# The row maximum of the attention scores and its scaling made by one VectorE operation

## The chip, the cores and the metric

The kernel runs on one core of a Trainium2 chip. The metric is the device time of one execution in microseconds; less is better. Before the change the median of three runs is 1622.26 us (1620.82 to 1622.88). The core has a matrix engine (TensorE, PE in the profile), a vector engine (VectorE, DVE), an activation engine (ScalarE, ACT), GpSimd (POOL) and a queue engine (SyncE, SP) that issues all of this kernel's DMAs. Matrix products land in PSUM; everything else on the chip lies in SBUF.

## The reference

Two sequences (x_prompt and x_sample, called A and B here) of 1024 tokens by 1024 features go through the same two layers. The first is a pooling mixer beside an attention with 8 query heads of 64 and 2 key/value heads; the second is a gated layer. What matters here is the softmax:

```python
s = jnp.einsum('bqkgd,bskd->bkgqs', q_blk, k, preferred_element_type=jnp.float32) * scale
p = jax.nn.softmax(s, axis=-1).astype(v.dtype)
return jnp.einsum('bkgqs,bskd->bqkgd', p, v)
```

For each query row the softmax needs the greatest of 1024 scores, subtracts it, takes the exponential and divides by the sum.

## The kernel before, in words

The attention works on pairs of heads: `attention(st, j, rate)` takes head pair j (0 to 3) of one sequence. In it, 8 token tiles (4 groups of two) and two heads make 16 score tiles of 128 queries by 1024 keys. Four pairs and two sequences make 128 score tiles. A's attention begins at about 90 us of the span and B's ends at about 880 us.

`scores` (L673 to L687) makes one tile. Four matmuls of 128x512 (L678) fill a PSUM tile `ps` of 128x1024 in f32; there are two such PSUM tiles (`ps_s`, L213). VectorE takes the maximum of each row (L684, `m`). ScalarE multiplies it by the negative scale `s_neg`, a [128, 1] operand (L685, `nb`). ScalarE then computes exp(scale * ps + nb) with the sum of each row as accumulator output (L686). `ps` is free for the next matmuls when L684 and L686 have read it.

`split` (L689 to L701) handles the tile before it: ScalarE scales the sum (L693), VectorE takes the reciprocal (L695), ScalarE writes the high half of the probabilities in f16 (L697), VectorE the low half (L698), and SyncE issues the DMA that transposes both (L699). `pv` (L703) multiplies them with the values on TensorE (L710) and VectorE evacuates the result (L714).

Between two score tiles `fill(rate)` takes chunks of other work from a list of fillers: the projections of this and the other sequence and the pooling mixer during A's attention, the output projection of A and the beginning of the second layer during B's. Their matmuls are in a helper, L399. Weight blocks are loaded in f32 by SyncE (L153) and split in two f16 halves by ScalarE (L169) and VectorE (L170); the buffers come out of one arena.

Two planners stand around this. `make_plan` (L76) gives each buffer of the arena its place: a first pass notes when each buffer is taken and freed, and the plan then places all of them in `ARENA` bytes per partition, seeking places whose last user is long gone. So a different arena size gives other places and other reuse. And the program is scheduled by the framework (L1060, `schedule_with_timeline_sim=True`), which sets the order on each engine by its own estimate of the timeline; that order is not always the order of the lines.

Of the kernel before, what the change touches and what calls it, by code (L numbers as in the profile page):

```python
# [13 lines left out]
BF16 = mybir.dt.bfloat16  # L14
I32 = mybir.dt.int32
AF = mybir.ActivationFunctionType
ALU = mybir.AluOpType
AX = mybir.AxisListType
PSUM = bass.MemoryType.PSUM

P = 128
L = 1024
# [7 lines left out]
PAD = 8  # L30
W_PAD = L + 2 * PAD
RING = 96
ARENA = 201 * 1024
GRAIN = 512


class Arena:
# [3 lines left out]
    def __init__(self, nc, pool, plan=None):  # L41
        self.tile = pool.tile([P, ARENA // 4], F32, name="arena")
        self.nc, self.plan = nc, plan
        self.spans, self.held, self.now = [], {}, 0.0
# [45 lines left out]
def tried(spans, order, end):  # L90
    placed, plan = [], [None] * len(spans)
    for i in order:
# [3 lines left out]
        holes, last = [], 0  # L96
        for lo, hi in clash + [(ARENA, ARENA)]:
            if lo - last >= g:
# [101 lines left out]
class Kernel:  # L200
    def __init__(self, ctx, tc, args, order, plan):
        self.nc, self.tc, self.order = tc.nc, tc, order
        self.__dict__.update(args)
        self.one = one = ctx.enter_context(tc.tile_pool(name="one", bufs=1))
        self.kept = one.tile([P, 640], F32, name="kept")
        self.kept_at = 0
        self.rings, self.role = {}, "misc"
        self.blocks = {}
        self.arena = Arena(tc.nc, one, plan)
        self.get, self.free = self.arena.get, self.arena.free  # L210
        self.diff = one.tile([P, 2, L], F32R, name="diff")
        self.pw = one.tile([P, 2, 4, P], F32R, name="pw")
        self.ps_s = ctx.enter_context(tc.tile_pool(name="ps_s", bufs=2, space=PSUM))  # L213
        self.ps_g = ctx.enter_context(tc.tile_pool(name="ps_g", bufs=3, space=PSUM))
        self.ps_o = ctx.enter_context(tc.tile_pool(name="ps_o", bufs=1, space=PSUM))
        dram = ctx.enter_context(tc.tile_pool(name="dram", bufs=1, space=bass.MemoryType.DRAM))
        self.x1 = [dram.tile([L, D], F32, name=f"x1_{s}") for s in range(2)]
        self.mixed = [dram.tile([8, P, L], F32, name=f"mixed_{s}") for s in range(2)]
        self.w = {"in_e": self.w_in_e, "out_e": self.w_out_e, "in_o": self.w_in_o, "out_o": self.w_out_o}
        self.fillers = deque()  # L220
        self.credit = 0
        self.turned = {}
# [437 lines left out]
    def attention(self, st, j, rate):  # L660

        nc = self.nc
        while not {("q", j), ("az", j)} <= st.done:
            cost, fn = self.fillers.popleft()
            fn()
            self.credit -= cost
        kv = j // 2
        out = self.get([P, L], F32)
        sz = st.az[j]["t"]
        sc = self.product(st.az[j]["d"], st.dv, 2.0 ** -15, tag="so")  # L670
        pts = {}

        def scores(tt, h):  # L673
            ps = self.ps_s.tile([P, L], F32, name="ps_s")
            for half in range(2):
                for a in range(2):
                    self.arena.now += 512
                    nc.tensor.matmul(out=ps[:, half * 512:half * 512 + 512], lhsT=st.qT[j][:, tt, h, :],  # L678
                                     rhs=st.kT[:, 4 * half:4 * half + 4, kv, a, :], start=a == 0, stop=a == 1)
            m = self.tiny([P, 1])  # L680
            nb = self.tiny([P, 1])
            p = self.pf.get()
            ss = self.tiny([P, 1])
            nc.vector.tensor_reduce(out=m, in_=ps, axis=AX.X, op=ALU.max)  # L684
            nc.scalar.activation(out=nb, in_=m, func=AF.Copy, scale=self.s_neg[:, 0:1])  # L685
            nc.scalar.activation(out=p, in_=ps, func=AF.Exp, scale=self.s_scale[:, 0:1], bias=nb[:, 0:1], accum_out=ss)  # L686
            return p, ss  # L687

        def split(tt, h, p, ss):  # L689
            if tt % 2 == 0:  # L690
                pts[tt // 2, h] = self.pt.get()
            s2 = self.tiny([P, 1])
            nc.scalar.activation(out=s2, in_=ss, func=AF.Copy, scale=2.0 ** -15)  # L693
            r = self.tiny([P, 1])
            nc.vector.reciprocal(out=r, in_=s2)  # L695
            hl = self.phl.get()
            nc.scalar.activation(out=hl[:, 0, :], in_=p, func=AF.Copy, scale=r[:, 0:1])  # L697
            nc.vector.scalar_tensor_tensor(out=hl[:, 1, :], in0=p, scalar=r[:, 0:1], in1=hl[:, 0, :], op0=ALU.mult, op1=ALU.subtract)  # L698
            nc.sync.dma_start_transpose(  # L699
                out=pts[tt // 2, h].rearrange("p a t n -> p (a t) n")[:, :, (tt % 2) * P:(tt % 2 + 1) * P],  # L700
                in_=hl.rearrange("p a n -> p (a n)"))  # L701

        def pv(g):  # L703
            ps = self.bank(self.ps_o)[:, 0:256]
            n = 0
            for t in range(NT):
                for a, b in self.PASSES:
                    for h in range(2):
                        self.arena.now += 128
                        nc.tensor.matmul(out=ps[h * HD:h * HD + HD, :], lhsT=st.v[:, a, t, kv * HD:kv * HD + HD],  # L710
                                         rhs=pts[g, h][:, b, t, :], start=n < 2, stop=n >= 6 * NT - 2)
                        n += 1
            cols = slice(g * 256, g * 256 + 256)
            nc.vector.scalar_tensor_tensor(out=out[:, cols], in0=ps, scalar=sc[:, 0:1], in1=sz[:, cols], op0=ALU.mult, op1=ALU.mult)  # L714

        prev = None
        for g in range(NT // 2):
            for h in range(2):
                for tt in (2 * g, 2 * g + 1):
                    with self.as_role("attention"):  # L720
                        cur = (tt, h) + scores(tt, h)
                        if prev:
                            split(*prev)
                    prev = cur
                    self.fill(rate)
                    if g and h == 1 and tt % 2 == 0:
                        pv(g - 1)
        with self.as_role("attention"):
            split(*prev)
        self.fill(rate)  # L730
        pv(NT // 2 - 1)
        self.amax(st.mam[:, 4 + j:5 + j], out)
        if j < 3:
            nc.sync.dma_start(out=self.mixed[st.s][4 + j], in_=out)
            self.free(out)
        else:
            st.mix[7] = out
        self.free(sz, st.qT.pop(j))
# [348 lines left out]
```

## Time and profile before

| | before |
|---|---|
| median of 3 runs | 1622.26 us |
| profiled execution, its time | 1619.84 us |
| profiled execution, its span | 1618.1 us |
| mean granted TensorE clock, share of full speed | 0.976 |
| PE, DVE, ACT busy over the span | 92%, 66%, 45% |

The span is the time from the first to the last instruction of the profiled execution; 1.7 us lie around it. The busy shares are averages over stages with different limits, so the prediction reads them by stretch.

### The profile page before, as it was taken

What the parts mean: (1) busy time and instruction counts of PE and PEld (TensorE: products, weight loads), DVE (VectorE), ACT (ScalarE), POOL (GpSimd) and SP (SyncE); (2) the same over time, 40 slices, a digit from 0 to 9 for tenths busy, and PEclk for the clock granted to TensorE, in tenths of its full rate; (3) what the DMA queues carried; (4) which work ended last, traced back from release to release, by engine and by line L of the source; (5) the groups of instructions that cost most, each with busy time, mean ns of one, the idle gap of its engine ahead of it and who ended that gap; (6) DMA issues with size and microseconds to landing.
All of it is one profiled execution on the core that took longest, in us unless ns stands there. A gap on an engine that the chain in (4) does not pass through costs nothing.

```text
span 1618.1 us, 28061 instructions
## 1 busy us (share of the span) xinstructions
PE 1496.5 (92%) x11751; PEld 1014.1 (63%) x11751; DVE 1061.8 (66%) x1613; ACT 729.0 (45%) x1121; POOL 117.3 (7%) x187
## 2 busy tenths in 40 slices
PE   2989998878799999999799999999999999998999
PEld 1754654557456787464478887554488554467888
DVE  7899999889897675788975854466650643345211
ACT  4367767767664364566755811133432521111000
POOL 2410000102000000000200100010000200000000
PEclk9999999889889999999899999999999999999999
DMA  9558688899948877675997643157210023114121
GB/s 252 116 118 161 150 148 183 186 210 194 213 87 213 211 156 151 144 154 133 224 260 164 186 125 98 40 157 167 81 40 1 27 66 117 46 66 137 60 85 53
DMA packets 497152, 217.69 MB, mean 135 GB/s; under 512 B 366337, under 2 KB 488705, under 8 KB 497025
## 3 DMA queue, kind: packets, MB, share of 16 engines
q1 hardware_dynamic: 497024, 215.90, 57.0%
q8 instruction: 92, 1.51, 0.4%
q14 instruction: 36, 0.29, 0.1%
HBM read 101.04 MB, written 24.12 MB: 77 GB/s over the span
## 4 chain that ended last, share of the span: by engine, by line
PE 57%; DVE 16%; DMA 11%; issue 4%; ACT 4%; POOL 1%; SPq 1%; DVEq 0%; ACTq 0%; POOLq 0%
PE bank L399 35%; PE ps_s L399 17%; DMA arena<-arena 4%; PE bank L710 3%; DVE arena L698 3%; DVE ring_attention L684 3%; PE ps_s L678 3%; DMA arena<-in_w_in_e 2%; DMA arena<-in_w_in_o 1%; DMA arena<-x 1%; ACT arena L686 1%; DVE ring_weights L252 1%; DVE arena L170 1%; DVE arena L756 1%; DVE arena L622 1%
## 5 line engine op out<-in xcount | busy, mean ns | idle before, releaser
L399 PEld LDWEIGHTS <-arena 128*128 128x128 f16 x9600 | 863.9, 99 | 434.1 <-DMA arena<-arena 25.6
L399 PE MATMUL bank<-arena 128*128 128x256 f16 (+2 forms) x8064 | 941.1, 277 | 31.8 <-ACT arena L169 12.7
L399 PE MATMUL ps_s<-arena 128*128 128x512 f16 x1536 | 338.1, 380 | 2.4 <-DVE arena L170 2.4
L169 ACT ACTIVATE arena<-arena,kept 128x1024 f16<-128x1024 f32 x108 | 121.4, 1142 | 281.1 <-DVE kept L281 126.2
L170 DVE SCALAR_TENSOR_TENSOR arena<-arena,kept 128x1024 f16<-128x1024 f32 x108 | 137.6, 1288 | 80.9 <-ACT arena L169 63.9
L698 DVE SCALAR_TENSOR_TENSOR arena<-arena,ring_attention 128x1024 f16<-128x1024 f32 x128 | 163.2, 1278 | 31.3 <-ACT arena L697 29.9
L684 DVE TENSOR_REDUCE ring_attention<-ps_s 128x1 f32<-128x1024 f32 x128 | 155.0, 1216 | 10.8 <-PE ps_s L678 10.5
L697 ACT ACTIVATE arena<-arena,ring_attention 128x1024 f16<-128x1024 f32 x128 | 145.5, 1141 | 36.0 <-DVE ring_attention L695 27.1
L678 PE MATMUL ps_s<-arena 128*128 128x512 f16 x512 | 136.8, 394 | 26.2 <-ACT arena L686 21.5
L686 ACT ACTIVATE arena<-ps_s,ring_attention,kept 128x1024 f32<-128x1024 f32 x128 | 153.7, 1201 | 8.4 <-DVE ring_attention L695 3.7
L784 DVE SCALAR_TENSOR_TENSOR arena<-bank,ring_dout,arena 128x512 f32<-128x512 f32 x64 | 47.9, 749 | 149.7 <-PE bank L399 149.7
L710 PE MATMUL bank<-arena 128*64 128x256 f16 x1536 | 107.7, 290 | 35.7 <-DMA arena<-arena 34.3
L710 PEld LDWEIGHTS <-arena 128*64 128x64 f16 x1536 | 90.2, 117 | 61.2 <-DMA arena<-arena 31.6
L252 DVE TENSOR_REDUCE ring_weights<-arena 128x1 f32<-128x1024 f32 x58 | 70.2, 1215 | 66.6 <-DMA arena<-in_w_in_o 29.4
L678 PEld LDWEIGHTS <-arena 128*128 128x128 f16 x512 | 47.9, 100 | 81.1 <-issue 38.6
L685 ACT ACTIVATE ring_attention<-ring_attention,kept 128x1 f32<-128x1 f32 x128 | 37.1, 290 | 131.4 <-DVE ring_attention L684 131.0
L364 DVE SCALAR_TENSOR_TENSOR arena<-arena,ring_norm 128x1024 f32<-128x1024 f32 x32 | 41.8, 1306 | 25.7 <-POOL ring_norm L318 22.7
L362 ACT ACTIVATE arena<-arena 128x1024 f32<-128x1024 f32 x32 | 33.7, 1054 | 53.1 <-DMA arena<-x 32.9
L903 DVE TENSOR_TENSOR arena<-arena 128x1024 f32<-128x1024 f32 x16 | 19.6, 1223 | 51.2 <-ACT arena L902 51.2
L838 ACT ACTIVATE arena<-bank,ring_dvv 128x256 f32<-128x256 f32 x64 | 26.7, 466 | 54.8 <-PE bank L399 53.9
L902 ACT ACTIVATE arena<-ps_s,ring_duz 128x1024 f32<-128x1024 f32 x16 | 17.7, 1109 | 66.8 <-PE ps_s L399 66.8
L365 ACT CAST arena<-arena 128x1024 f16<-128x1024 f32 x32 | 33.2, 1037 | 23.8 <-DVE arena L364 22.3
(104 smaller groups left out, 883.6 us busy)
## 6 DMA issues: line engine op xcount, KB each, us to landing
arena<-in_w_in_o SPq DMA_DIRECT2D x48, 512.0 KB, 4.4
arena<-in_w_in_e SPq DMA_DIRECT2D x36, 512.0 KB, 4.8
arena<-in_w_out_e SPq DMA_DIRECT2D x16, 512.0 KB, 4.6
x<-arena SPq DMA_DIRECT2D x32, 256.0 KB, 3.0
arena<-x SPq DMA_DIRECT2D x16, 512.0 KB, 4.8
arena<-x SPq DMA_DIRECT2D x32, 256.0 KB, 3.0
out<-arena SPq DMA_DIRECT2D x32, 256.0 KB, 2.1
mixed<-arena SPq DMA_DIRECT2D x14, 512.0 KB, 4.1
```

The source lines that it names most:

```text
L169: nc.scalar.activation(out=hi, in_=raw, func=AF.Copy, scale=s[:, 0:1])
L170: nc.vector.scalar_tensor_tensor(out=lo, in0=raw, scalar=s[:, 0:1], in1=hi, op0=ALU.mult, op1=ALU.subtract)
L252: self.nc.vector.tensor_reduce(out=out, in_=in_, axis=axis, op=ALU.max, apply_absolute_value=True)
L364: nc.vector.scalar_tensor_tensor(out=x, in0=x, scalar=r[:, 0:1], in1=gain[0], op0=ALU.mult, op1=ALU.mult)
L399: self.nc.tensor.matmul(out=o, lhsT=l, rhs=r, start=first and i == 0, stop=last and i == n - 1)
L678: nc.tensor.matmul(out=ps[:, half * 512:half * 512 + 512], lhsT=st.qT[j][:, tt, h, :], rhs=st.kT[:, 4 * half:4 * half + 4, kv, a, :], star ...
L684: nc.vector.tensor_reduce(out=m, in_=ps, axis=AX.X, op=ALU.max)
L686: nc.scalar.activation(out=p, in_=ps, func=AF.Exp, scale=self.s_scale[:, 0:1], bias=nb[:, 0:1], accum_out=ss)
L697: nc.scalar.activation(out=hl[:, 0, :], in_=p, func=AF.Copy, scale=r[:, 0:1])
L698: nc.vector.scalar_tensor_tensor(out=hl[:, 1, :], in0=p, scalar=r[:, 0:1], in1=hl[:, 0, :], op0=ALU.mult, op1=ALU.subtract)
L710: nc.tensor.matmul(out=ps[h * HD:h * HD + HD, :], lhsT=st.v[:, a, t, kv * HD:kv * HD + HD], rhs=pts[g, h][:, b, t, :], start=n < 2, stop=n ...
L784: nc.vector.scalar_tensor_tensor(out=res, in0=ps.rearrange("p (t n) -> p t n", t=2), scalar=box["d"][:, 0:1], in1=res, op0=ALU.mult, op1=A ...
```

## The change

VectorE no longer makes a plain maximum. One `tensor_scalar` multiplies each score by the negative scale, takes the lesser of the product and 3e38 (which changes nothing), and keeps the least of the results in its accumulator output, which is `nb`. As `s_neg` is negative, the least product is the product of the greatest score. The elementwise result goes to a scratch tile of 128x1024 in bf16 that nobody reads; its 2 KB per partition are taken from the arena. The ScalarE multiplication (L685) goes. The [128, 1] tile `m` goes too.

```diff
-ARENA = 201 * 1024
+ARENA = 199 * 1024
...
+        self.scratch = one.tile([P, L], BF16, name="scratch")
...
-            m = self.tiny([P, 1])
             nb = self.tiny([P, 1])
             p = self.pf.get()
             ss = self.tiny([P, 1])
-            nc.vector.tensor_reduce(out=m, in_=ps, axis=AX.X, op=ALU.max)
-            nc.scalar.activation(out=nb, in_=m, func=AF.Copy, scale=self.s_neg[:, 0:1])
+            nc.vector.tensor_scalar(out=self.scratch, in0=ps, scalar1=self.s_neg[:, 0:1], scalar2=3.0e38, op0=ALU.mult, op1=ALU.min, accum_out=nb)
             nc.scalar.activation(out=p, in_=ps, func=AF.Exp, scale=self.s_scale[:, 0:1], bias=nb[:, 0:1], accum_out=ss)
```

## Rows read from the trace of the kernel before

**Rows 1.** Page, part 1: busy us, share of the span, instructions.
```profile
PE 1496.5 (92%) x11751; PEld 1014.1 (63%) x11751; DVE 1061.8 (66%) x1613; ACT 729.0 (45%) x1121; POOL 117.3 (7%) x187
```

**Rows 2.** Stretch, its length; busy PE, PEld, DVE, ACT, POOL; granted clock; DMA.
```profile
90.00:290.00 200.00, 184.55 (x1373) 103.08 (x1371) 188.20 (x314) 142.45 (x246) 11.94 (x20) 0.99 0.77 155
290.00:480.00 190.00, 160.96 (x1458) 107.04 (x1457) 168.41 (x256) 134.00 (x224) 25.72 (x35) 0.91 0.89 181
480.00:880.00 400.00, 373.73 (x3098) 261.63 (x3097) 300.00 (x425) 229.16 (x381) 20.67 (x38) 0.98 0.79 179
880.00:1618.00 738.00, 722.45 (x5294) 499.30 (x5292) 334.23 (x465) 187.81 (x225) 28.38 (x48) 0.99 0.30 88
```

**Rows 3.** The chain of waits from 90 to 880 us, shares by line.
```profile
by line: PE bank L399 25.3%; DMA arena<-arena 7.8%; issue 7.8%; DVE arena L698 6.1%; PE bank L710 5.8%; DVE ring_attention L684 5.7%; PE ps_s L678 5.7%; DMA arena<-in_w_in_e 4.2%; ACT arena L686 2.9%; DVE arena L622 1.9%; DMA arena<-in_w_ou
```

**Rows 4.** The chain in order of time: start, us, what; L684's and L685's first and last.
```profile
90.92 1.13 DVE ring_attention L684
...
181.16 1.23 DVE ring_attention L684
...
182.41 0.30 ACT ring_attention L685
...
756.02 0.19 ACT ring_attention L685
...
818.50 1.14 DVE ring_attention L684
```

**Rows 5.** Groups by line: xcount | busy us, mean ns | idle before, releasers.
```profile
L684 DVE TENSOR_REDUCE ring_attention<-ps_s 128x1 f32<-128x1024 f32 x128 | 155.0, 1216 | 10.8 <-PE ps_s L678 10.5
L685 ACT ACTIVATE ring_attention<-ring_attention,kept 128x1 f32<-128x1 f32 x128 | 37.1, 290 | 131.4 <-DVE ring_attention L684 131.0
L686 ACT ACTIVATION_READ_ACCUMULATOR arena<-ps_s,ring_attention,kept 128x1 f32 x128 | 24.5, 191 | 0.0
L695 DVE RECIPROCAL ring_attention<-ring_attention 128x1 f32<-128x1 f32 x128 | 19.9, 157 | 19.6 <-ACT ring_attention L693 19.3
L591 DVE SCALAR_TENSOR_TENSOR arena<-arena,bank 128x512 f32<-128x512 f32 x32 | 21.7, 679 | 1.4 <-ACT arena L590 1.4
L884 DVE SCALAR_TENSOR_TENSOR arena<-bank,kept,arena 128x512 f32<-128x512 f32 x32 | 22.8, 748 | 31.3 <-PE bank L399 31.2
L753 DVE TENSOR_SCALAR arena<-arena,kept 128x1024 f16<-128x1024 f32 x16 | 11.2, 747 | 0.1
```

**Rows 6.** Timeline from 242 us: start, us, engine, line, operation.
```profile
243.00 1.22 DVE L684 TENSOR_REDUCE ring_attention<-ps_s 128x1 f32<-128x1024 f32 x1
244.13 1.27 DVE L698 SCALAR_TENSOR_TENSOR arena<-arena,ring_attention 128x1024 f16<-128x1024 f32 x1
244.58 1.20 ACT L686 ACTIVATE arena<-ps_s,ring_attention,kept 128x1024 f32<-128x1024 f32 x1
245.68 0.19 ACT L686 ACTIVATION_READ_ACCUMULATOR arena<-ps_s,ring_attention,kept 128x1 f32 x1
245.77 1.14 ACT L169 ACTIVATE arena<-arena,kept 128x1024 f16<-128x1024 f32 x1
```

**Rows 7.** DVE's runs of L684 in the first stretch.
```profile
90.00:290.00 200.00, 49.76 (x41) 0.99 0.77 155
```

**Rows 8.** Waits: who waited for whom, us in total, times, longest.
```profile
PE ps_s L678 <- ACT arena L686: 21.5, 14, 3.0
SPq L699 <- DVE ring_attention L684: 55.6, 14, 6.7
SPq L153 <- DVE arena L170: 86.0, 13, 21.3
```

**Rows 9.** Timeline at 569 us, and the chain's weight loads between 90 and 880 us.
```profile
569.70 2.35 DVE L684 TENSOR_REDUCE ring_attention<-ps_s 128x1 f32<-128x1024 f32 x2
93.27 5.10 DMA arena<-in_w_in_e
...
827.60 4.16 DMA arena<-in_w_in_o
```

## The prediction

> **What bounds the kernel now.** I read the page's totals first, then the busy time by stretch, then the chain of waits, then the groups and a piece of the timeline for prices. Over the whole span TensorE is busy 92% and VectorE 66% [rows 1], which would make VectorE a bystander. The stretches say otherwise. From 90 to 290 us, the first part of A's attention, VectorE is busy 188.2 of 200 us, and from 290 to 480 us 168.4 of 190; in B's attention (480 to 880 us) it is 300 of 400, with TensorE at 373.7; after 880 us TensorE has 722 of 738 us to itself [rows 2]. So 128 score tiles lie in a region of 790 us, where A's half leaves VectorE 11.8 + 21.6 = 33 us of idle time and B's half leaves TensorE 26 us. In the last stretch the change touches nothing but places of buffers.
>
> The chain of waits from 90 to 880 us is mixed: TensorE's fillers have 25%, transposes 8%, and the reduction L684 has 5.7%, which is 45 us of 790 [rows 3]. In order of time the chain holds L684 in 47 pieces, the first at 90.9 and the last at 818.5 us; 38 of them are whole runs of 1.07 to 1.24 us. It holds L685, the multiplication that goes, in 19 pieces from 182.4 to 756.0 us, 4.1 us together (ten of about 0.30, the rest shorter) [rows 4]. That is the quantity to see: ScalarE's 128 runs of 290 ns are 37.1 us of busy time [rows 5], but only 4.1 us of it is on the path.
>
> **The change part by part.** *What ScalarE loses.* 128 x 290 ns = 37.1 us of ScalarE work [rows 5]. ScalarE is busy 142 of 200, 134 of 190 and 229 of 400 us in the three stretches [rows 2], so most of this is idle time traded for idle time. On the path it is worth the 4.1 us above, and one hop of about 0.02 us (the gap from 182.39 to 182.41 us [rows 4]) in each of the ten places where the chain goes from L684 straight into L685: 0.2 us. I take -4.3 us, and keep 0 as the small end, because a parallel wait may be right behind. At the other end, the exp that frees a PSUM tile starts about 0.3 us earlier, and TensorE waited for that exp 14 times [rows 8]: 14 x 0.3 = 4.2 us more, were VectorE to charge nothing for it.
>
> *What VectorE gains in work.* No row shows a `tensor_scalar` that reads PSUM with an accumulator output, so it is bounded from its neighbours. The reduction over 1024 takes 1216 ns and the next operation starts 1.13 us after it began (243.00 to 244.13) [rows 6]. The operand `s_neg` is read per partition: the same operation on 512 elements in which PSUM takes part takes 679 ns with a constant (L591) and 748 ns with a [128, 1] operand (L884) [rows 5], so I add 0.06 to 0.07 us, and take 0.06. The accumulator has to be brought out. VectorE shows no such step anywhere in this trace; ScalarE does, as an instruction of its own of 191 ns [rows 5], which started 1.10 us into its exp and let the next operation start 0.09 us later (244.58, 245.68, 245.77) [rows 6]. VectorE's nearest [128, 1] operation, the reciprocal, takes 157 ns [rows 5]. Low end: the accumulator comes out within the operation, 0, and a score tile costs 0.06 us more. High end: no overlap at all, 1.28 + 0.19 = 1.47 us where the step was 1.13, so 0.34 more. The row it is nearest to is ScalarE's, with 0.09 to 0.19 us: I take 0.13, and so 0.19 us more per tile, 24 us of VectorE's time over 128 tiles. There is an end below nothing too: a `tensor_scalar` from SBUF over 1024 elements takes 747 ns (L753) [rows 5]. If the new one ran at that rate from PSUM, a tile would cost 0.47 - 0.13 = 0.34 us less; it is priced among the rivals.
>
> The Trainium skill (VectorE: DVE Perf Modes, Two Vector instructions with no wait between them) says that an operation that also writes out its accumulator is two instructions, the main one and an accumulator read. ScalarE's rows agree in kind; no VectorE row here shows it. By that rule the low end of 0.06 us falls away and the sum is the one I take or above it; by the low end alone the forecast would be no change.
>
> *Where that work lies.* On the chain: 38 whole runs x 0.19 = +7.2 us. Beside the chain: in the first stretch VectorE makes 41 of the 128 reductions [rows 7], 12 of the 38 are there, so 29 are not on the chain; but they would add 29 x 0.19 = 5.5 us to an engine with 11.8 us idle [rows 2]. VectorE's order is fixed, and SyncE sits for 55.6 us, 14 times, at a transpose (L699) until an L684 has run [rows 8]; so what is late on VectorE makes transposes late, and with them L710. I count half of it: +2.8 us. Elsewhere I count nothing beside the chain: the fillers cover it, and if they don't, the other 61 runs off the chain (128 - 41 - 26) cost up to 61 x 0.19 = 11.6 us.
>
> *Waits.* The exp now waits for VectorE itself and not for L685; behind it on ScalarE stand the same instructions as stood behind L685. The scratch tile is written by VectorE alone, so no other engine waits for it. No DMA is added or moved.
>
> *Arena and order.* 2 KB of 201 go, so the planner places every buffer anew, and the framework orders the engines anew (already now it puts two reductions of consecutive tiles one behind the other at 569.70 us, which the lines don't have [rows 9]). Both can gain or lose. Weight loads are the place: 12 of them are on the chain between 90 and 880 us, 3.6 to 5.6 us each, 55 us together [rows 9], and their issue waited 86 us, 13 times, for L170 to have read the buffer before [rows 8]. One load more or less on the path is some 4.5 us either way. I take 0 for the value and keep both ends.
>
> *Sum.* -4.3 + 7.2 + 2.8 = +5.7 us against the profiled execution's 1619.84 us, which gives 1625.5; the median of the runs is 2.4 us above it, so the prediction is 1622.26 + 5.7 = 1628 us. With VectorE's low end it is -4.3 + 38 x 0.06 + 29 x 0.06 / 2 = -1.1 us; with its high end -4.3 + 38 x 0.34 + 29 x 0.34 / 2 = +13.5 us.
>
> **The rivals.** *ScalarE's relief decides (faster).* The accumulator costs VectorE nothing, and each exp, 0.3 us earlier, frees its PSUM tile earlier: -4.3 - 4.2 + 38 x 0.06 = -6.2 us, 1616 us. For it speak the 21.5 us that TensorE waited for L686 [rows 8], which is the largest wait of L678 for an engine; against it, that VectorE at 94% [rows 2] can't start the reduction earlier. It wins over the forecast from a price below about 0.08 us a tile on VectorE. Chance 0.22.
>
> *Both sides cancel (no change).* The longer operation still hands over sooner: 1.19 + 0.19 + 0.02 us from its start to the exp against 1.23 + 0.02 + 0.30 + 0.02 before [rows 4]. At the ten places where the chain goes through L685 that is already in the sum; if fillers cover the 28 others by half, the result is -4.3 + 10 x 0.19 + 14 x 0.19 = 0.3 us, 1622.5 us. Chance 0.22.
>
> *The new places decide (slower).* Two weight loads or transposes more on the path, 9 to 10 us, beside the forecast's +5.7: 1637 us. For it speaks that the issues already wait for buffers; against it, that it may fall the other way. Chance 0.12.
>
> *The new operation runs at the double rate (much faster).* 0.34 us less on 38 + 14 runs and 4.3 on ScalarE: -17.7 - 4.3 = -22 us, 1600 us. For it speaks L753; against it, that L884 and L591 with an operand in PSUM take 1.3 to 1.5 ns an element, as an operation at the single rate and its start would. The Trainium skill (VectorE: DVE Perf Modes, Why PSUM operands drop a tier) says that a 32-bit operand in PSUM keeps an operation at one element a cycle; no row here has a `tensor_scalar` from PSUM to show it. Chance 0.04.
>
> **How the numbers follow.** The forecast has the rest, 0.40, with its own range of 1623 to 1634 us. A measurement of this kernel can tell about 0.2%, 3.2 us, from no change. Faster: 0.22 + 0.04 = 0.26. Same: 0.22 and about 0.05 of the forecast, whose lower edge lies inside that band, 0.27. Slower: 0.35 + 0.12 = 0.47. The range is 1612 to 1639: it leaves out the double rate, and the tails of the first and third rivals, some 0.15 to 0.2 together.
>
> **What would show it.** Right: a VectorE operation of about 1.28 us at L681 and beside it a second, short one, 128 times; VectorE's busy time up by some 20 us or more; ScalarE's down by about 37; VectorE above 95% from 90 to 290 us, and TensorE's idle time there up, not down. Wrong: no second instruction, or an exp that starts less than 1.3 us after the VectorE operation with TensorE's waits for L686 gone; or VectorE as forecast but the difference lying after 880 us or in weight loads, which would be the places. A time under 1619 us would say that ScalarE was on the path by more than its pieces of the chain.

## The result and the profile after

The changed kernel takes 1647.18 us (median of four runs, 1646.47 to 1647.48) against 1622.57 us for the kernel before in the same session. The ratio is 1.015, interval 1.0135 to 1.0165: 24.6 us slower. The forecast of 1628 us had the sign right, but the time lies outside its range, which ended at 1639.

The profiled execution took 1647.43 us, with a span of 1645.7 us and a mean granted TensorE clock of 0.961 (before 1618.1 us and 0.976). First the page's totals, which answer to [rows 1]:

```profile
PE 1508.8 (92%) x11751; PEld 1019.5 (62%) x11751; DVE 1071.1 (65%) x1741; ACT 698.4 (42%) x993; POOL 115.7 (7%) x187
```

TensorE executes the same 11751 matmuls and is busy 12.3 us longer with them. The other 15.3 us of the 27.6 are TensorE idle. VectorE has 128 instructions more and only 9.3 us more busy time; ScalarE has 128 less and 30.6 us less.

The groups by line, which answer to L684 to L686 in [rows 5] (lines are shifted by one: the exp is L685 now, the low half's L698 is L697, the helper's L399 is L400):

```profile
L684 DVE TENSOR_SCALAR_CACHE_REDUCE scratch<-ps_s,kept 128x1024 bf16<-128x1024 f32 x128 | 163.3, 1275 | 12.7 <-PE ps_s L679 12.0
L684 DVE DVE_READ_ACCUMULATOR scratch<-ps_s,kept 128x1 f32 x128 | 10.5, 82 | 0.0
L685 ACT ACTIVATE arena<-ps_s,ring_attention,kept 128x1024 f32<-128x1024 f32 x128 | 153.6, 1200 | 136.3 <-DVE scratch L684 127.4 <-DVE arena L697 4.5 <-DVE ring_attention L694 2.9
```

The new operation is two instructions on VectorE, 1275 and 82 ns, as the prediction said in kind. The timeline shows what they cost a neighbour; it answers to [rows 6]. Three dots stand for rows of other engines that are left out:

```profile
338.98 1.27 DVE L684 TENSOR_SCALAR_CACHE_REDUCE scratch<-ps_s,kept 128x1024 bf16<-128x1024 f32 x1
...
340.18 0.08 DVE L684 DVE_READ_ACCUMULATOR scratch<-ps_s,kept 128x1 f32 x1
340.18 1.28 DVE L697 SCALAR_TENSOR_TENSOR arena<-arena,ring_attention 128x1024 f16<-128x1024 f32 x1
340.30 1.20 ACT L685 ACTIVATE arena<-ps_s,ring_attention,kept 128x1024 f32<-128x1024 f32 x1 [1.32 <-DVE scratch L684]
```

The accumulator is read from 340.18 us on, 1.20 us after the operation began, and the next VectorE operation starts in the same instant. So the step from one operation to the next is 1.20 us where it was 1.13 [rows 6]: 0.07 us a tile. The 128 tiles of the two traces agree: the median step is 1.203 us for 1.134, and in 107 of them the next operation starts with the read. And the exp starts 1.32 us after VectorE began, where it was 1.23 + 0.02 + 0.30 + 0.02 = 1.57 us [rows 4].

These rows account for at most 128 x 0.07 = 9 us of VectorE's time, most of it beside other work, and not for 25 us. The stretches, against [rows 2], show where the time is lost:

```profile
90.00:290.00 200.00, 194.66 (x1410) 109.29 (x1409) 187.83 (x358) 129.77 (x199) 13.89 (x18) 0.97 0.76 153
290.00:480.00 190.00, 143.69 (x1292) 96.54 (x1290) 159.08 (x271) 125.08 (x191) 23.04 (x35) 0.83 0.93 187
480.00:880.00 400.00, 371.19 (x3025) 252.63 (x3024) 306.51 (x475) 209.47 (x315) 22.15 (x41) 0.96 0.75 168
880.00:1645.00 765.00, 745.89 (x5516) 519.47 (x5513) 348.35 (x489) 199.84 (x245) 26.01 (x48) 0.99 0.31 90
```

From 90 to 290 us TensorE issues even more than before (1410 matmuls for 1373). From 290 to 480 us it falls back: 143.7 us busy for 161.0, 1292 matmuls for 1458. The mean granted clock of that stretch is 0.83 of 2.4 GHz (before 0.91), so more of it ran at the lower level, 1.2 GHz, with TensorE idle 46 us of 190. VectorE too does less there, 159.1 for 168.4 us. The last of the 128 reductions starts at 894.2 us where it was 872.2: 22 of the 27.6 us are lost by the end of attention, and 15.8 of them by the 64th reduction (438.9 us for 423.1), where A's score tiles end. The largest wait of the score matmuls for an engine has doubled (before 21.5 us, 14 times [rows 8]):

```profile
PE ps_s L679 <- ACT arena L685: 42.6, 19, 6.4
```

Two things changed, then: the operation, and the 2 KB that the scratch tile takes from the arena, which moves the buffers and gives the framework another problem to order. The experiments take them apart.

### The profile page after: what moved, and what is told of

It reads as the page before. It is cut to its first block, busy times and chain, and to the rows that moved or that the text cites. A ratio compares the mean times of both kernels' runs of the same rounds, so it can differ in the third digit from the quotient of the medians.

```text
span 1645.7 us, 28017 instructions
## 1 busy us (share of the span) xinstructions
PE 1508.8 (92%) x11751; PEld 1019.5 (62%) x11751; DVE 1071.1 (65%) x1741; ACT 698.4 (42%) x993; POOL 115.7 (7%) x187
## 4 chain that ended last, share of the span: by engine, by line
PE 54%; DVE 19%; DMA 14%; issue 5%; ACT 5%; POOL 2%; SPq 2%; DVEq 0%; ACTq 0%; POOLq 0%
PE bank L400 34%; PE ps_s L400 15%; DMA arena<-arena 4%; DVE scratch L684 4%; DMA arena<-in_w_in_e 3%; DVE arena L697 3%; PE bank L709 3%; DVE arena L170 2%; PE ps_s L679 2%; DMA arena<-in_w_in_o 2%; ACT arena L685 1%; ACT arena L169 1%; DVE arena L365 1%; DMA arena<-in_w_out_e 1%; DVE ring_weights L253 1%
## 5 line engine op out<-in xcount | busy, mean ns | idle before, releaser
L400 PEld LDWEIGHTS <-arena 128*128 128x128 f16 x9600 | 869.3, 99 | 442.4 <-DMA arena<-arena 25.6
L400 PE MATMUL bank<-arena 128*128 128x256 f16 (+2 forms) x8064 | 948.2, 279 | 31.1 <-ACT arena L169 13.2
L400 PE MATMUL ps_s<-arena 128*128 128x512 f16 x1536 | 337.7, 380 | 8.2 <-ACT arena L169 8.1
L685 ACT ACTIVATE arena<-ps_s,ring_attention,kept 128x1024 f32<-128x1024 f32 x128 | 153.6, 1200 | 136.3 <-DVE scratch L684 127.4
L679 PE MATMUL ps_s<-arena 128*128 128x512 f16 x512 | 142.1, 404 | 49.9 <-ACT arena L685 42.6
L697 DVE SCALAR_TENSOR_TENSOR arena<-arena,ring_attention 128x1024 f16<-128x1024 f32 x128 | 163.1, 1278 | 16.7 <-ACT arena L696 16.6
L684 DVE TENSOR_SCALAR_CACHE_REDUCE scratch<-ps_s,kept 128x1024 bf16<-128x1024 f32 x128 | 163.3, 1275 | 12.7 <-PE ps_s L679 12.0
L253 DVE TENSOR_REDUCE ring_weights<-arena 128x1 f32<-128x1024 f32 x58 | 70.5, 1216 | 68.8 <-DMA arena<-in_w_in_o 32.6
L367 DVE TENSOR_TENSOR arena<-arena 128x1024 f16<-128x1024 f32 x32 | 39.9, 1250 | 4.9 <-ACT arena L366 4.9
L316 POOL TENSOR_SCALAR ring_norm<-ring_norm 128x1 f32<-128x1 f32 x32 | 12.8, 400 | 422.6 <-ACT arena L363 418.3
```

The source lines that it names most:

```text
L253: self.nc.vector.tensor_reduce(out=out, in_=in_, axis=axis, op=ALU.max, apply_absolute_value=True)
L400: self.nc.tensor.matmul(out=o, lhsT=l, rhs=r, start=first and i == 0, stop=last and i == n - 1)
L684: nc.vector.tensor_scalar(out=self.scratch, in0=ps, scalar1=self.s_neg[:, 0:1], scalar2=3.0e38, op0=ALU.mult, op1=ALU.min, accum_out=nb)
```

## The experiments

Ratios are to the kernel before on the same chip, with the 95% interval.

### The places alone

```diff
-ARENA = 201 * 1024
+ARENA = 199 * 1024
```

That is the kernel before, with the maximum and the product on ScalarE as they were.

> The kernel before with only the arena cut to 199 KB; TENSOR_REDUCE and the ScalarE product stay, no scratch tile. If the new operation is what costs (theory O), this stays at 1622 us (within 3). If the new places of the buffers, and the order that follows from them, cost it (theory P), this is at 1640 to 1650 us, as the changed kernel. A share of both would lie between, and says how much each has.

1.0175 (1.0151 to 1.0199), 1653.72 us. The arena by itself costs all that the change costs. The same stretches of its profile:

```profile
90.00:290.00 200.00, 193.11 (x1399) 107.42 (x1397) 184.65 (x316) 140.81 (x242) 11.78 (x17) 0.98 0.76 149
290.00:480.00 190.00, 150.35 (x1369) 102.92 (x1367) 158.49 (x236) 131.66 (x222) 24.79 (x35) 0.88 0.94 192
480.00:880.00 400.00, 360.13 (x2903) 243.47 (x2902) 295.88 (x417) 215.59 (x361) 26.18 (x41) 0.95 0.74 166
```

It is like the changed kernel in kind: ahead in the first stretch, TensorE down to 150.4 us in the second, a lower granted clock. It does not lose the time in the same place, though: its 64th reduction starts 8.4 us later than before (431.5 us) and its last 26.4 us later (898.6), so that two thirds of its loss lie in B's attention, where TensorE is busy 360.1 of 400 us for 373.7. Its score matmuls wait more too, without the new operation:

```profile
PE ps_s L678 <- ACT arena L686: 34.2, 15, 5.0
```

Three more sizes, each the kernel before with one number changed. For 203 KB the 2 KB come from rings of small values (next experiment).

```diff
-ARENA = 201 * 1024
+ARENA = 198 * 1024    # the others: 200, 203
```

> The kernel before with an arena of 198 KB: another draw of places. If an arena of less than 201 KB costs because there is less of it, this is slower than e1. If places and order are a lottery, it lies anywhere within some 10 us of e1 or of 1622 us.

198 KB: 1.0173 (1.0151 to 1.0195), 1653.86 us.

> The kernel before with an arena of 200 KB. The planner places all buffers at the first attempt, as at 201 and 203 KB, and 72 of 593 lie elsewhere than at 201. At 199 and 198 KB two 4 KB buffers of a weight block (taken at 49% of the run) find no hole; they are put ahead of the others and all is placed again, so that 340 of 593 lie elsewhere. Theory R (that second attempt costs, not the space): 1622 to 1630 us. If time goes with space: about half of e1's +28, 1636 to 1642 us.

200 KB: 1.0046 (1.0028 to 1.0064), 1636.06 us.

> The kernel before with an arena of 203 KB (the 2 KB from rings whose slots are never used twice). If it is the amount of space that counts, this is at 1622 us or faster. If each plan is a draw, and that of 201 KB a good one, this is slower by 10 to 30 us, like 199 and 198 KB.

203 KB: 1.0004 (0.999 to 1.0018), 1626.74 us. So it is not a slope: 201 and 203 KB agree, 200 costs 0.5%, 199 and 198 cost 1.7%. (198 is no independent draw: one buffer of 593 lies elsewhere than at 199.)

### The operation without the loss of memory

The scratch tile's 2 KB come out of rings of [128, 1] values whose slots are never used twice, and the arena stays at 201 KB. The plan is then the same as before, buffer for buffer; only the operation differs.

```diff
+            size = RING if self.role in ("attention", "norm", "rope", "misc", "weights") else 32
...
-ARENA = 199 * 1024
+ARENA = 201 * 1024
```

> The changed kernel with the arena left at 201 KB; the 2 KB for the scratch tile come from the rings of [128, 1] values whose slots are never used twice. The plan of places is that of the kernel before. Theory O: 1640 to 1650 us, as the changed kernel. Theory P: near the prediction's price of the operation alone, 1622 to 1630 us.

1.0057 (1.0036 to 1.0078), 1636.89 us: about a third of the loss. But the framework orders the engines anew around the changed operation, so this isn't yet the operation's own price. The same at 198 KB, to be read against 198 KB with the old operations:

> The changed kernel's operation with an arena of 198 KB. Against e3 it gives the operation's effect under another draw of places: theory O says +20 to +25 us over e3, theory P +0 to +8 us, and a lottery of the order says any difference, of either sign.

1.0151 (1.0131 to 1.0172) for 1.0173: here the operation seems to gain 0.2%, and the changed kernel itself against the places alone gives 1.015 for 1.0175, the same sign; both differences lie within the intervals. So the order had to be held fixed.

### The operation in the old order

The program is scheduled with the old operations; afterwards each of the 128 reductions is replaced in its place on VectorE by the new operation, with the waits on its own engine that the scratch tile needs. In the first kernel ScalarE still makes its product; in the second the product goes as well, and the exp takes over its wait. The lines are those of the second kernel; in the first, the traces show every instruction of TensorE, ScalarE and GpSimd in the order of the kernel before:

```diff
+            if type(ins).__name__ == "InstTensorReduce" and ins.ins[0].memref.startswith("ps_s"):
+                l[i] = mybir.InstTensorScalarPtr(
...
+                    ins=(ins.ins[0], by, mybir.ImmediateValue(dtype=F32, value=3.0e38)),
+                    outs=(scratch, out), op0=ALU.mult, op1=ALU.min)
```

> The kernel before with its places and its order on every engine kept, instruction by instruction; only the 128 reductions are replaced, after the order is set, by the new multiply-and-keep-the-least operation (by -0.5, with its scratch tile and its waits on itself). The ScalarE multiplication stays and multiplies by twice the scale. So only VectorE's price is added, 0.06 us and the 0.08 us accumulator read of the changed kernel's profile. Theory O (the operation's own price makes e2's +11 us): +8 to +14 us over before. Theory S (the new order makes it): +0 to +6 us, the prediction's sum for VectorE alone being 38 x 0.14 + 29 x 0.14 / 2 = 7 us at most.

1.0024 (1.001 to 1.0038), 1629.29 us, that is +3.9 us. Here VectorE multiplies by a constant and ScalarE still multiplies by the scale, so only VectorE pays.

> As e5, and the ScalarE multiplication is taken out too, its waits moved to the exp: the whole change of the computation, with the places and the order of the kernel before. The prediction's sum without any new order is +2 to +4 us (0.14 us a tile on the chain, less 4.3 us of ScalarE). Theory S: at or below 1622 us within 3. Theory O: +8 to +14 us, as e2.

1.0006 (0.9995 to 1.0018), 1628.01 us for 1626.02. Against the kernel before it in this pair, ScalarE's product is worth 0.18%, some 2.9 us. The whole change, without new places and a new order, is no change that can be measured. VectorE's groups have the durations of the changed kernel, and the handover on VectorE is the same:

```profile
244.52 1.28 DVE L685 TENSOR_SCALAR_CACHE_REDUCE arena<-ps_s,kept 128x1024 bf16<-128x1024 f32 x1
...
245.72 0.08 DVE L685 DVE_READ_ACCUMULATOR arena<-ps_s,kept 128x1 f32 x1
245.72 1.28 DVE L699 SCALAR_TENSOR_TENSOR arena<-arena,ring_attention 128x1024 f16<-128x1024 f32 x1
```

The exp starts 1.40 us after the operation began, where it was 1.32 in the changed kernel (1.41 and 1.32 in the median), so that this kernel takes a little less of ScalarE's relief than it could.

The wait of the score matmuls is back at its old size, and so is TensorE from 290 to 480 us (160.1 us busy for 161.0 [rows 2]):

```profile
PE ps_s L679 <- ACT arena L687: 20.1, 14, 3.0
```

```profile
290.00:480.00 190.00, 160.09 (x1438) 106.75 (x1439) 166.88 (x280) 127.33 (x194) 27.57 (x38) 0.89 0.90 182
```

VectorE is busier in this stretch than in the changed kernel (166.9 us for 159.1), with the same operation. So the operation, as such, doesn't make that stretch slow.

### What about the places

At 203, 201 and 200 KB the planner's first attempt fits. At 199 and 198 KB two buffers of 4 KB, halves of one weight block, find no hole. The planner puts each at the front of its list and places everything again, twice; in the end 340 of 593 buffers lie elsewhere than at 201 KB (72 at 200 KB, 21 at 203). Two experiments on this theory (R: the restart is the loss). First another set of places at 201 KB, by another value of the planner's limit for how long a place should have been free, without a restart; 275 buffers lie elsewhere:

```diff
-SLACK = 0.035
+SLACK = 0.040
```

> The kernel before with 201 KB as it is, but with the planner's cap on the age it seeks at 0.040 of the run where it was 0.035, so that it places buffers otherwise in the same space. Space counts: within 5 us of 1622. A draw: anywhere up to 1655 us.

1.0049 (1.0033 to 1.0066). Then 199 KB, where a buffer that finds no hole moves only 20 places ahead in the list; 178 buffers lie elsewhere:

```diff
+        was = order.index(stuck)
         order.remove(stuck)
-        order.insert(next((n for n, i in enumerate(order) if spans[i][2] < 16384), 0), stuck)
+        order.insert(max(was - 20, next((n for n, i in enumerate(order) if spans[i][2] < 16384), 0)), stuck)
```

> The kernel before with 199 KB, where a buffer that found no hole moves only 20 places ahead in the planner's order, not to the front: 178 of 593 buffers lie elsewhere than at 201 KB. Theory R: well below e1's 1650 us, 1625 to 1640. If 199 KB is too little whatever the planner does: 1645 to 1655 us.

1.0093 (1.0068 to 1.0118), 1644.16 us: about half of the 1.75%, between the two times that were expected. It is another set of places, and sets that need no restart differ by up to 0.5% (200 KB, and 201 KB with the other limit). So the restart goes along with the largest losses; what it costs by itself is not shown.

> The changed kernel, 199 KB and all, with that planner. Theory R: from 1647 us down to what the operation with a new order costs, 1628 to 1640 us. If the change's +25 us is not the second attempt: 1645 to 1650 us.

The changed kernel with that planner: 1.0121 (1.0101 to 1.0141), 1648.35 us. It gains 0.3% against the change as it is, not the 0.8% that the places gave.

At the other two sets of places, the new operation:

> The changed kernel with 200 KB (1 KB more from rings never used twice), the scratch tile kept. The planner's first attempt succeeds. Theory R: near e2, 1630 to 1640 us, and against e9 it shows the operation with a free order once more.

200 KB: 1.0048 (1.0026 to 1.0069) for 1.0046.

> The changed operation at the places of e8 (201 KB, the planner's cap on age at 0.040). Against e8's +0.5%: if the operation by itself were slow, +10 us more; if the order that the framework finds for it is a draw, -8 to +12 us.

The other places at 201 KB: 1.0014 (0.9998 to 1.0031) for 1.0049.

### Is it the late loads of B's input

At 199 KB the loads of B's input come later, here the first and the last of the eight in the kernel of the places alone (before: at 241.75 and 358.13 us):

```profile
280.51 0.90 SPq L358 DMA_DIRECT2D arena<-in_x_sample  x1
...
381.32 0.87 SPq L358 DMA_DIRECT2D arena<-in_x_sample  x1
```

Theory L: these loads hold back B's projections, which are the fillers between A's score tiles. One kernel has edges that are to put loads 4 to 7 ahead of the transposes of tiles 2 to 5 in the order, at 199 KB; one delays them in the kernel before; one does the first in the changed kernel.

```diff
+        if src is self.xs[1] and tt in (4, 5, 6, 7):
+            self.tc.add_manual_dep(self.turned[tt - 2].ins, load.ins.name, ...)
```

```diff
-        with self.behind(tt - AHEAD if early else None):
+        late = {3: 2, 4: 2, 5: 3, 6: 3, 7: 6}.get(tt) if src is self.xs[1] else None
+        with self.behind(tt - AHEAD if early else late):
```

> The kernel of e1 (199 KB, the old operations) with four order-only edges on SyncE: the loads of x_sample tiles 4 to 7 stand ahead of the transposes of tiles 2 to 5, as they do in the kernel before. Theory L (the late loads are the loss): most of e1's +28 us goes, 1625 to 1635 us. If they are only a symptom of a later schedule: 1645 to 1655 us.

1.0155 (1.0132 to 1.0178) for 1.0175: nothing that can be told apart. But the loads did not come earlier. They run from 282.55 to 382.40 us, where they ran from 280.51 to 381.32, and the last still stands behind the transpose of tile 5 (377.63 us):

```profile
382.40 0.71 SPq L358 DMA_DIRECT2D arena<-in_x_sample  x1
```

What moved are the transposes (that of tile 2 from 329.64 to 356.37 us) and not the loads, so the run doesn't tell what earlier loads would bring.

> The kernel before, places and all, with order-only edges on SyncE that put the loads of x_sample tiles 3 and 4 behind the transpose of tile 2, 5 and 6 behind that of 3, and 7 behind that of 6, as they stand with 199 KB. Theory L: +15 to +25 us, 1637 to 1647. If they are a symptom: within 8 us of before.

1.0042 (1.0024 to 1.006), 6.8 us: late loads cost a little at the good places. Here they did move: the last is issued at 373.63 us, two thirds of the way from 358.13 to 381.32, for a quarter of the loss.

> The changed kernel with the edges of e13. Theory L: 1625 to 1635 us. Symptom: 1643 to 1650 us.

1.0179 (1.0144 to 1.0213) for 1.015, with the last load only 6 us earlier (377.14 us for 383.19). That late loads are the whole loss is unlikely after the second kernel. How much of it they are stays open, since no run at 199 KB brought them back to their old times.

### Waits or order

The last pair was to have the places of 201 and of 199 KB with one and the same order, so that only the places differ (340 of 593 buffers), and with them what each buffer has to wait for. For this the framework's estimate of the timeline is switched off; the two expectations below take it that each engine then runs its instructions in the order of the lines.

```diff
-        with tile.TileContext(nc, schedule_with_timeline_sim=True) as tc:
+        with tile.TileContext(nc, schedule_with_timeline_sim=False) as tc:
```

> The kernel before with the framework's estimate of the timeline switched off, so that each engine runs its instructions in the order of the program's lines; arena 201 KB. It is the base of a pair: the other kernel of the pair has the same instructions in the same order on every engine, with the places of a 199 KB arena. Both theories expect this one to be slower than before (the lines' order was not what the kernel was measured with), between +0.5 and +5%. What counts is the difference to the other.

1.0493 (1.0471 to 1.0515), 1705.77 us.

> The same kernel with ARENA = 199 KB: the order on each of the five engines is the same, instruction by instruction, and only the places of the buffers, and so the waits for their earlier users, differ. Theory O (the places cost time through the order that the framework finds): within 0.3% of the other of the pair, since no order changes. Theory W (the places cost time through waits for buffers that come free later): about 1.2 to 1.8% slower than the other of the pair, as at the free order (+1.75%). Between 0.5 and 1.0%: both.

1.0458 (1.0439 to 1.0478), 1699.43 us: with the bad places it is 0.3% faster (1.0458 / 1.0493 = 0.9967). But the two orders are not the same. VectorE's traces part at 68 us, 201 KB first, then 199 KB:

```profile
68.51 0.28 DVE L292 TENSOR_REDUCE ring_weights<-bank 128x1 f32<-128x128 f32 x1
68.71 1.21 DVE L252 TENSOR_REDUCE ring_weights<-arena 128x1 f32<-128x1024 f32 x1
```

```profile
68.91 0.28 DVE L292 TENSOR_REDUCE ring_weights<-bank 128x1 f32<-128x128 f32 x1
69.11 0.20 DVE L308 TENSOR_SCALAR ring_dkv<-kept 128x1 f32<-128x1 f32 x1
```

Counted by operation, tiles and shape, VectorE has the same instruction at 658 of 1613 places in its order, and ScalarE at 580 of 1121. Between the kernel before and the places alone it is 517 and 411. So the framework orders anew without its estimate too, and the pair doesn't separate the waits from the order.

What it does show is that the price of a set of places is not fixed. With the estimate the places of 199 KB cost 1.75%; without it they cost nothing. The estimate is worth 4.9% at 201 KB (1.0493 against 1) and 2.8% at 199 KB (1.0458 against 1.0175).

## Why the prediction was wrong

**The step that failed.** "I take 0 for the value and keep both ends" of "Arena and order". The places are worth +1.75% with the old operation, and the changed kernel's +1.5% is no more than that. The end kept for them was one weight load on the path, "some 4.5 us either way", and the rival made of it was two of them, 9 to 10 us. It measured 28 us by the places alone (0.0175 x 1625.8). The rival "the new places decide (slower)" is what happened, with a chance of 0.12 and a price of a third. The price was sized as one event on the path. What the runs show in its place is a new order on every engine with the new places, and a loss spread over all of attention: 8.4 us by the 64th tile and 26.4 by the last, for the places alone. What the framework's estimate gains falls from 4.9 to 2.8%. Whether the time goes to the poorer order itself or to waits for buffers in it is not shown.

The sign of the forecast was right by luck: its +5.7 us were the operation's, and the operation alone measured 1 us.

**VectorE's price.** The pointer operand was taken at 0.06 us and cost 1275 - 1216 = 59 ns. The accumulator was taken at 0.13 us by ScalarE's rows; its read takes 82 ns and all of it overlaps the next operation, so that the step grew by 0.07 us in place of 0.19. With 0.07 VectorE's part of the sum is 38 x 0.07 + 29 x 0.07 / 2 = 3.7 us; the kernel in which only VectorE pays measured +0.24%, 3.9 us (1.6 to 6.2). With ScalarE's -4.3 the whole is -0.6 us, no change; in the old order it measured +0.06%, 1 us. So the working for the operation was sound, with one term, the 0.19 us, at nearly three times its size, and "both sides cancel" holds for the operation alone.

The Trainium skill (VectorE: DVE Perf Modes, Two Vector instructions with no wait between them) was used to say that the low end of 0.06 us falls away. In kind this case's trace agrees, with 128 reads of 82 ns; in price the step is the low end after all, to 0.01 us, since the read stands beside the next operation.

**The order around the operation.** With the framework free to order, the new operation against the old at the same places gave +0.57, -0.35, +0.02, -0.25, -0.22, +0.28 and +0.24% (201 KB, the other draw at 201, 200, 199, 198, the gentler planner, the early loads). The mean is 0.04%, and each is a new order (199 and 198 KB are nearly one draw). Only +0.57 and -0.35% are clear of their intervals. The prediction had no term for that; its size is up to half a per cent either way.

**ScalarE's relief.** ScalarE lost 30.6 us of busy time where 37.1 was expected. The other 6.5 are in the counting: the durations of its instructions add up to 791.7 us before and 755.0 after, 36.7 less, and busy time counts once what overlaps. "It wins over the forecast from a price below about 0.08 us a tile": the price was 0.07 and it did not win. In the old order TensorE still waited 20.1 us, 14 times, for the exp (21.5 and 14 before [rows 8]), so of the rival's further 4.2 us there came 1.4. The chain's -4.3 us was nearly right: taking the product out measured -0.18%, 2.9 us, where the two runs' intervals allow 0 to 6.

**The signs to look for.** Right: the two instructions and no double rate (1275 ns where 747 would have shown it). Wrong: "VectorE's busy time up by some 20 us or more"; it is 9.3, since the read overlaps the next operation. Wrong: "VectorE above 95% from 90 to 290 us, and TensorE's idle time there up"; it is 187.8 of 200 us, 94%, and TensorE's idle time went down from 15.5 to 5.3 us. Wrong too: that the places would show "after 880 us or in weight loads". After the last score tile the changed kernel loses 5.6 us; 22 are lost in attention. Someone who went by that sign would have put the loss down to the operation.

**What stays open.** Whether the new places cost their time through the order that comes with them or through waits for buffers that come free later: no two runs have one order and these two sets of places. That the places of 199 KB would hurt in the good order of 201 KB was not tried. Which part of attention pays differs from run to run, and how much of it the late loads of B's input are was not settled.

## What to carry to other kernels

An edit that takes memory from a planned arena, in a program that a framework orders, is two edits: price the new plan apart, by running the old operations with the smaller arena, and look whether the planner's first attempt still fits (the largest losses here were behind a restart, but 200 KB fitted at once and cost 0.5%). Take a scratch tile's bytes from somewhere that the plan doesn't see where that can be done. And before an operation is blamed or praised for a few tenths of a per cent, run it at several sets of places or in a frozen order; here the same edit measured between -0.35 and +0.57%, by the order it was drawn in. And where an experiment is to hold an order or move a transfer, look in its trace whether it did: here two were to and did not.

## What had not been expected of the hardware

VectorE's read of its accumulator costs its engine almost nothing where another operation stands behind it: 82 ns, begun 1.20 us into an operation of 1.275 us, in the same instant as the next operation (340.18 us). The step is 0.069 us longer than the plain reduction's, and the operation itself is 0.059 us longer. ScalarE's, of 191 ns, let the next operation start 0.09 us later [rows 6]. A scratch tile written by VectorE alone is not free of waits: at this line VectorE now has 62 semaphore instructions of 21 ns, which the plain reduction did not have; in the built program they wait for VectorE itself, whose earlier write of the tile must be over. And 12.3 of the 27.6 us that the profiled execution lost are the same 11751 matmuls taking longer, at a mean granted clock of 0.961 instead of 0.976; where TensorE idled most (290 to 480 us, 46 us of 190) the clock was lowest, 0.83.
